# Attention scores as 64-deep products in row halves, and a division moved behind the value product

## The chip, the core and the metric

The kernel runs on one core of one Trainium2 chip. The core has TensorE (PE, with its weight loads as PEld), VectorE (DVE), ScalarE (ACT), GpSimd (POOL) and SyncE (SP), which issues DMA. The metric is the device time of one execution in microseconds, as a median of several. One execution was also recorded by the profiler; the rows below are from that one.

## What is computed

One inference step of a mixer layer: a normalised and modulated input goes through one projection into branches; two of them are a short convolution and a spatial gate, the third is a neighbourhood attention over a 32 x 64 grid of 2048 latent tokens, whose queries also see 128 cached context keys, and 128 prompt tokens that see their own 128 keys. There are 8 heads of 64. The branches are gated, joined and projected back. What matters here is the attention and its gate (without the indexing):

```python
s_loc = einsum(q, k_window) * ATTN_SCALE
s_loc = where(valid, s_loc + bias, NEG_INF)
s_ctx = einsum(q, ctx_k) * ATTN_SCALE
p = softmax(concatenate([s_loc, s_ctx], axis=-1), axis=-1)
out = einsum(p_loc, v_window) + einsum(p_ctx, ctx_v)
yc = out.reshape(bn, n, C_W) * silu(gc)
```

## The kernel before

All matrix products are done in float16 with a high and a low half of each factor, three products for one (high x high, high x low, low x high).

**Stages.** Up to 410 us the kernel normalises the input, computes the spatial gate and the values, and splits the weights. From there to 960 us it works through a list of jobs, one projection of 128 output channels each (`proj`, 24 products per tile of 512 tokens): for each of four head pairs `q`, `k` and the gate `gc`, and between them the convolution branch (`xa`, `ca`, and `ba` with `ga`, the convolution job). From 960 us it does the output projection.

**Attention between the projections.** A head pair's attention has 17 units: 16 blocks of 8 x 16 queries (a window of 352, 480 or 384 keys and the 128 context keys) and the prompt tokens. The steps of a unit don't run in a loop of their own. They are posted with a due time on a modelled clock (`post`), and each projection product advances that clock (`tick`); a step is emitted, in the order of its due time, between two projection products. The table `T` holds the times: `pace` is the distance of two units (6.0, 6.0, 4.9 and 4.7 us for the four head pairs), `a_half` the half pace between the two heads, `a_step` the delays of the steps behind the scores, `a_val` the delay of the value products behind the transposing DMA (5.7, 7.5, 6.2 and 5.6 us). `drain` emits what is still open of a given tag at once. Every engine works through its own instructions in the order in which they were emitted.

**Steps of one head of a unit.** `scores`: the stationary factor `QS` holds the high half of the queries in 64 rows and the low half in the other 64, and `KH` and `KL` hold the keys' halves twice, in both row halves; so a product over 128 rows with `KH` and one with `KL` make all scores (L1028 for the context, L1031 for the window). The second copy of the keys is made by DMA from SBUF to SBUF (L1249, L1250). VectorE adds the bias table `TB` and takes the maximum (L1043). `expo` on ScalarE writes the exponentials in float32 with their sum (L1052), `norm` on VectorE takes the reciprocal (L1055, L1056), `high` on ScalarE writes the normalised probabilities in float16 into one of three buffers `PH` (L1059), `low` on VectorE the rest (L1062), and `turn` issues a transposing DMA from SyncE's queue (L1068). `values` makes the products with `VW` and `v_ctx` in two column halves of the array, one for each head (L1087), and VectorE combines the result with the gate `sgc` (L1095). GpSimd makes the bias tables (`make_tables`, L1002) and the convolution (`conv`, L1182 and L1185).

## Time and profile before

| | |
|---|---|
| median of three runs | 1187.61 us (1185.17 to 1192.42) |
| the profiled execution, its own time | 1188.24 us |
| its span, first to last instruction | 1186.2 us |
| TensorE busy | 1069.7 us, 90% of the span |
| VectorE busy | 843.5 us, 71% |
| ScalarE busy | 447.3 us, 38% |
| GpSimd busy | 346.2 us, 29% |

The shares are means over stages with different limits, so what a change in the attention is worth has to be read from 410 to 926 us, where the attention runs. A busy TensorE counts a product until its results are out; how far apart two products begin tells how much of the queue one takes.

### The profile page before, as it was taken

The page shows a single profiled execution, that of the slowest core. Times are in us where ns is not written, and L with a number is a line of the kernel's source. Part 1 is how long each engine was busy: PE and PEld are TensorE (multiplying, and loading weights), DVE is VectorE, ACT ScalarE, POOL GpSimd, SP SyncE. Part 2 cuts the span into 40 slices and gives each one's busy share as a digit, 9 for nine tenths or more (in the row PEclk, how much of TensorE's full clock was granted, in tenths as well). Part 3 has the DMA queues.
Part 4 walks back from the last instruction along what each step waited for, and adds up shares of the span by engine and source line. Part 5 has one row for each costly group of instructions (what it writes and reads, how often), then busy time and mean ns, then how long its engine had stood idle before and what let it go on. Part 6 is the DMA issues. An engine that isn't in the chain of part 4 may idle for free. (4 is left out here: it accounts for less than half of the span.)

```text
span 1186.2 us, 21036 instructions
## 1 busy us (share of the span) xinstructions
PE 1069.7 (90%) x8044; PEld 681.4 (57%) x8044; DVE 843.5 (71%) x2071; ACT 447.3 (38%) x758; POOL 346.2 (29%) x346
## 2 busy tenths in 40 slices
PE   5588989889968999999999999999988999888885
PEld 1377866477754455554545445545544477776774
DVE  4678866665562389954898549973899658777877
ACT  1432322223332266543655436753666321121111
POOL 0145655200002122102662022300325414334434
PEclk9699999989988999999999999999999999999998
DMA  9713104168957238754666746757476663433341
GB/s 330 260 43 103 59 10 142 54 211 294 308 185 197 77 74 147 130 127 102 113 145 122 152 105 125 150 125 150 97 136 119 198 211 107 144 123 106 120 129 54
DMA packets 254356, 165.50 MB, mean 140 GB/s; under 512 B 163600, under 2 KB 224808, under 8 KB 254256
## 3 DMA queue, kind: packets, MB, share of 16 engines
q1 hardware_dynamic: 254256, 164.16, 53.6%
q8 instruction: 63, 1.03, 0.4%
q14 instruction: 37, 0.30, 0.1%
HBM read 88.06 MB, written 36.21 MB: 105 GB/s over the span
## 5 line engine op out<-in xcount | busy, mean ns | idle before, releaser
L548 PE MATMUL pj<-h_hi,wring 128*128 128x512 f16 (+1 forms) x1280 | 336.2, 349 | 9.2 <-DMA wring<-wj_d 9.2
L548 PEld LDWEIGHTS <-wring 128*128 128x128 f16 x2400 | 211.7, 98 | 224.1 <-DMA wring<-wj_d 9.3
L548 PE MATMUL pj<-h_lo,wring 128*128 128x512 f16 (+1 forms) x640 | 217.9, 349 | 0.0
L1319 PE MATMUL ps<-wo,yh 128*128 128x512 f32 (+1 forms) x840 | 193.5, 390 | 21.0 <-DVE yh L1129 21.0
L1319 PEld LDWEIGHTS ps<-wo,yh 128*128 128x128 f32 x840 | 153.8, 188 | 60.5 <-DVE yh L1129 27.0
L1062 DVE SCALAR_TENSOR_TENSOR PH<-pt,sm,PH 128x608 f16<-128x608 f32 (+3 forms) x136 | 155.3, 1142 | 2.6 <-ACT PH L1059 2.4
L1002 POOL TENSOR_TENSOR TB<-raw,msk 128x480 f32<-128x480 f32 (+2 forms) x96 | 96.2, 1010 | 187.6 <-DVE sm L1043 187.6
L1059 ACT ACTIVATE PH<-pt,sm 128x608 f16<-128x608 f32 (+3 forms) x136 | 99.9, 734 | 95.1 <-ACT pt L1052 62.3
L1052 ACT ACTIVATE pt<-pt,sm,scal 128x608 f32<-128x608 f32 (+2 forms) x128 | 108.3, 846 | 57.6 <-DVE sm L1048 54.0
L1043 DVE CUSTOM_DVE_ANT_0 pt<-s,TB 128x608 f32<-128x608 f32 (+2 forms) x128 | 93.3, 729 | 11.2 <-PE s L1031 10.0
L558 PE MATMUL vvps<-wV,h_hi 128*128 128x256 f16 x544 | 94.0, 277 | 3.6 <-DVE vt L923 3.6
L558 PEld LDWEIGHTS <-h_hi 128*128 128x128 f16 x816 | 82.0, 102 | 23.1 <-issue 11.1
L548 PE MATMUL p<-h_hi,wring 128*128 128x512 f16 (+1 forms) x320 | 85.9, 352 | 1.9 <-DVE th L565 1.9
L1343 ACT ACTIVATE r<-r,omv 128x1024 f32<-128x1024 f32 x16 | 19.9, 1244 | 177.0 <-issue 141.1
L548 PEld LDWEIGHTS <-wB 128*128 128x128 f16 x768 | 63.4, 98 | 24.7 <-issue 1.3
L558 PE MATMUL vvps<-wV,h_lo 128*128 128x256 f16 x272 | 75.3, 277 | 0.0
L1344 POOL TENSOR_TENSOR r<-r,gam 128x1024 f32<-128x1024 f32 x16 | 38.2, 2388 | 126.4 <-ACT r L1343 126.4
L548 PE MATMUL ups<-h_hi,wB 128*128 128x128 f16 (+2 forms) x448 | 70.8, 267 | 0.3 <-DVE wB L238 0.3
L986 POOL TENSOR_SCALAR raw<-raw,scal 128x528 f32<-128x528 f32 x8 | 5.5, 704 | 220.2 <-DVE scal L189 165.8
L1129 DVE TENSOR_TENSOR yh<-yf,yh 128x1024 fp32r<-128x1024 f32 x17 | 41.0, 2410 | 35.2 <-ACT yh L1128 35.2
L1222 DVE SCALAR_TENSOR_TENSOR KL<-pj,scal,KH 64x512 f16<-64x512 f32 (+1 forms) x40 | 26.8, 670 | 54.1 <-ACT KH L1221 53.9
L496 POOL TENSOR_TENSOR h_lo<-hf,h_hi 128x512 f16<-128x512 f32 x34 | 39.9, 1179 | 74.9 <-DMA bsb<-in_b_spatial_dram 42.2
(214 smaller groups left out, 1712.0 us busy)
## 6 DMA issues: line engine op xcount, KB each, us to landing
wa<-in_w_ada_dram SPq DMA_DIRECT2D x24, 512.0 KB, 7.4
wraw<-in_w_in_dram SPq DMA_DIRECT2D x20, 512.0 KB, 5.7
wj_d<-wsp SPq DMA_DIRECT2D x40, 256.0 KB, 6.3
wring<-wj_d SPq DMA_DIRECT2D x20, 512.0 KB, 5.7
yf<-y_d SPq DMA_DIRECT2D x17, 512.0 KB, 5.6
xt<-in_x_sample_dram SPq DMA_DIRECT2D x16, 512.0 KB, 5.0
VW<-v_d SPq DMA_DIRECT2D x64, 128.0 KB, 5.1
xr<-in_x_sample_dram SPq DMA_DIRECT2D x16, 512.0 KB, 4.1
```

The lines of the kernel that those rows point to most:

```text
L496: G.tensor_tensor(out=h_lo[:, k0:k0 + g, t0:t0 + n], in0=hv, in1=hi, op=ALU.subtract)
L548: PE.matmul(out=ps, lhsT=w(a, k) if callable(w) else w[:, a, k, :], rhs=mov(b, k), start=(k == 0 and i == 0), stop=(k == KB - 1 and i == 2))
L558: PE.matmul(out=ps, lhsT=a[:, k, i * P:(i + 1) * P], rhs=w[:, b, k, :], start=(k == 0 and q == 0), stop=(k == KB - 1 and q == 2))
L1002: G.tensor_tensor(out=TB[:, tslot(u) + h, P:P + n], in0=raws[h][:, off:off + n], in1=msk[:, mo:mo + n], op=ALU.add)
L1043: V.tensor_tensor_reduce(out=pt[:, :w], in0=src, in1=TB[:, tslot(u) + h, 0:w], op0=ALU.add, op1=ALU.max, scale=1.0, scalar=-3e38, accum_ou ...
L1052: S.activation(out=pt[:, :w], in_=src, func=AF.Exp, bias=sm[:, 1:2], scale=st_["isig"], accum_out=sm[:, 2:3])
L1059: S.activation(out=pb[:, 0:w], in_=pt[:, :w], func=AF.Copy, scale=sm[:, 3:4])
L1062: V.scalar_tensor_tensor(out=pb[:, wp:wp + w], in0=pt[:, :w], scalar=sm[:, 3:4], in1=pb[:, 0:w], op0=ALU.mult, op1=ALU.subtract)
L1129: V.tensor_tensor(out=yh[:, 1], in0=yf, in1=yh[:, 0].bitcast(F32), op=ALU.subtract)
L1222: V.scalar_tensor_tensor(out=KL[a, h, t0:t0 + n], in0=ps[a], scalar=ckk[a], in1=KH[a, h, t0:t0 + n], op0=ALU.mult, op1=ALU.subtract)
L1319: PE.matmul(out=ps, lhsT=yh[:, a, k, :], rhs=wo[:, b, k, f0:f1], start=(k == 0 and q == 0), stop=(k == KB - 1 and q == 2))
L1344: G.tensor_tensor(out=r, in0=r, in1=gam, op=ALU.mult)
```

## The change

Queries and keys are kept once each, both heads of a pair one above the other in the 128 rows, as `QH`, `QL`, `KH`, `KL`. The scores of a unit are made for both heads together, each in three products over the 64 rows of its half of the array; the two heads' products alternate. The second copy of the keys and its DMAs go, and the copies out of the projections for Q and K cover 128 partitions in one operation in place of two of 64.

The probabilities aren't normalised any more before the value product. The exponent gets ln(2 to the power of 14) added; `high` is an exponential that writes float16, `expo` makes the same in float32 with the sum, and `low` is their difference, on GpSimd for the first head of a pair and on VectorE for the second. Per unit there is one reciprocal of both sums; GpSimd spreads it over a 128x128 tile `rq`, TensorE transposes that behind the value products, VectorE multiplies it with the gate (`gq`) and that with the value products. The modelled clock counts three passes for the scores of a unit, and `a_step` has four delays in place of five.

```diff
-    a_step=(700.0, 700.0, 2100.0, 2750.0, 3700.0),
+    a_step=(700.0, 750.0, 2700.0, 3300.0),
...
+LN14 = 14.0 * float(np.log(2.0))
...
-    QS = ap.tile([P, 2, TOK], F16, name="QS")
-    KH = ap.tile([P, 2, TOK + CTX], F16, name="KH")
-    KL = ap.tile([P, 2, TOK + CTX], F16, name="KL")
+    QH = ap.tile([P, TOK], F16, name="QH")
+    QL = ap.tile([P, TOK], F16, name="QL")
+    KH = ap.tile([P, TOK + CTX], F16, name="KH")
+    KL = ap.tile([P, TOK + CTX], F16, name="KL")
...
+                post(T['a_start'][hp] + u * pace, lambda u=u: self.scores(u), ("as", hp, u))
                 for h in range(2):
-                    post(T['a_start'][hp] + (u + T['a_half'] * h) * pace, lambda u=u, h=h: self.scores(u, h), ("as", hp, u))
-
-        def scores(self, u, h):
-            i = 2 * u + h
-            drain(("a", self.hp, i - T['a_guard']), ("at", self.hp, u))
-            tg = ("a", self.hp, i)
-            sm = ap.tile([P, 4], F32, name="sm", bufs=8)
-            s = aps.tile([P, 2, 512], F32, name="s", tag="s", bufs=2)
+                    post(T['a_start'][hp] + (u + T['a_half'] * h) * pace, lambda u=u, h=h: self.soft(u, h), ("as", hp, u))
+
+        def scores(self, u):
+            drain(("a", self.hp, 2 * u - T['a_guard']), ("at", self.hp, u))
+            n = 0
             if u < 16:
                 rb, j = UNITS[u]
                 nr = RB_NROW[rb]
                 n = 32 * nr
-                q = QS[:, h, u * P:(u + 1) * P]
-                for e, kk in enumerate((KH, KL)):
-                    PE.matmul(out=s[:, 0, 384:512], lhsT=q, rhs=kk[:, h, TOK:TOK + CTX], start=(e == 0), stop=(e == 1))
-                for e, kk in enumerate((KH, KL)):
-                    win = kk[:, h, RB_ROW0[rb] * 64:(RB_ROW0[rb] + nr) * 64].rearrange("p (r c) -> p r c", c=64)
-                    PE.matmul(out=s[:, 1, 0:n], lhsT=q, rhs=win[:, :, COL0[j]:COL0[j] + 32], start=(e == 0), stop=(e == 1))
-            else:
-                n = 0
-                q = QS[:, h, LAT:TOK]
-                for e, kk in enumerate((KH, KL)):
-                    PE.matmul(out=s[:, 0, 384:512], lhsT=q, rhs=kk[:, h, LAT:TOK], start=(e == 0), stop=(e == 1))
-            now[0] += 2 * (P + n) / 2.4
+            t0 = u * P
+            s = [aps.tile([P, 2, 512], F32, name="s", tag="s", bufs=2) for h in range(2)]
+            pairs = ((QH, KH), (QL, KH), (QH, KL))
+            for e, (q, kk) in enumerate(pairs):
+                for h in range(2):
+                    a = slice(64 * h, 64 * h + 64)
+                    k0 = TOK if u < 16 else LAT
+                    PE.matmul(out=s[h][:, 0, 384:512], lhsT=q[a, t0:t0 + P], rhs=kk[a, k0:k0 + CTX], start=(e == 0), stop=(e == 2))
+            if u < 16:
+                for e, (q, kk) in enumerate(pairs):
+                    for h in range(2):
+                        a = slice(64 * h, 64 * h + 64)
+                        win = kk[a, RB_ROW0[rb] * 64:(RB_ROW0[rb] + nr) * 64].rearrange("p (r c) -> p r c", c=64)
+                        PE.matmul(out=s[h][:, 1, 0:n], lhsT=q[a, t0:t0 + P], rhs=win[:, :, COL0[j]:COL0[j] + 32],
+                                  start=(e == 0), stop=(e == 2))
+            now[0] += 3 * (P + n) / 2.4
+            self.ss[u] = s
...
+            if h == 0:
+                self.sums[u] = ap.tile([P, 4], F32, name="sums", bufs=5)
+            total = self.sums[u]
+            s = self.ss[u][h]
...
-            V.tensor_scalar(out=sm[:, 1:2], in0=sm[:, 0:1], scalar1=st_["isig"], scalar2=-1.0, op0=ALU.mult, op1=ALU.mult)
+            V.tensor_scalar(out=sm[:, 1:2], in0=sm[:, 0:1], scalar1=st_["nisig"], scalar2=LN14, op0=ALU.mult, op1=ALU.add)
             pb = PH[:, i % 3]
 
+            def high():
+                S.activation(out=pb[:, 0:w], in_=src, func=AF.Exp, bias=sm[:, 1:2], scale=st_["isig"])
+
             def expo():
-                S.activation(out=pt[:, :w], in_=src, func=AF.Exp, bias=sm[:, 1:2], scale=st_["isig"], accum_out=sm[:, 2:3])
-
-            def norm():
-                V.tensor_scalar(out=sm[:, 2:3], in0=sm[:, 2:3], scalar1=2.0 ** -14, scalar2=None, op0=ALU.mult)
-                V.reciprocal(out=sm[:, 3:4], in_=sm[:, 2:3])
-
-            def high():
-                S.activation(out=pb[:, 0:w], in_=pt[:, :w], func=AF.Copy, scale=sm[:, 3:4])
+                S.activation(out=pt[:, :w], in_=src, func=AF.Exp, bias=sm[:, 1:2], scale=st_["isig"], accum_out=total[:, h:h + 1])
 
             def low():
-                V.scalar_tensor_tensor(out=pb[:, wp:wp + w], in0=pt[:, :w], scalar=sm[:, 3:4],
-                                       in1=pb[:, 0:w], op0=ALU.mult, op1=ALU.subtract)
+                (G if h == 0 else V).tensor_tensor(out=pb[:, wp:wp + w], in0=pt[:, :w], in1=pb[:, 0:w], op=ALU.subtract)
+                if h == 1:
+                    V.reciprocal(out=total[:, 2:4], in_=total[:, 0:2])
+                    r = ap.tile([P, P], F32, name="rq", bufs=4)
+                    for e in range(2):
+                        G.tensor_scalar(out=r[:, 64 * e:64 * e + 64], in0=ones[:, 0:64], scalar1=total[:, 2 + e:3 + e], scalar2=1.0,
+                                        op0=ALU.mult, op1=ALU.mult)
+                    self.rs[u] = r
 
             def turn():
                 drain(("av", self.hp, u - T['av_guard']))
@@ -1070,12 +1090,13 @@
                 if h == 1:
                     post(T['a_val'][self.hp], lambda: self.values(u, [self.ts.pop((u, e)) for e in range(2)], wp // P, n), ("av", self.hp, u))
 
-            for f, at in zip((expo, norm, high, low, turn), T['a_step']):
+            for f, at in zip((high, expo, low, turn), T['a_step']):
...
-            o = aps.tile([P, P], F32, name="o", tag="o")
+            o = aps.tile([P, 2, P], F32, name="o", tag="o")
+            rt, o = o[:, 1], o[:, 0]
...
+            PE.transpose(rt, self.rs.pop(u), ident)
             now[0] += nch * 3 * 80.0
+            t0 = u * P
+            gq = ap.tile([P, P], F32, name="gq", bufs=2)
+            V.scalar_tensor_tensor(out=gq, in0=rt, scalar=st_["cpv"], in1=sgc[:, t0:t0 + P], op0=ALU.mult, op1=ALU.mult)
             if u < 16:
                 rb, j = UNITS[u]
                 if j == 0:
                     self.ys = yst.tile([P, 8, 64], F32, name="yc", tag="yst")
-                V.scalar_tensor_tensor(out=self.ys[:, :, j * 16:j * 16 + 16], in0=o.rearrange("p (r c) -> p r c", c=16),
-                                       scalar=st_["cpv"], in1=sgc[:, u * P:(u + 1) * P].rearrange("p (r c) -> p r c", c=16),
-                                       op0=ALU.mult, op1=ALU.mult)
+                V.tensor_tensor(out=self.ys[:, :, j * 16:j * 16 + 16], in0=o.rearrange("p (r c) -> p r c", c=16),
+                                in1=gq.rearrange("p (r c) -> p r c", c=16), op=ALU.mult)
...
-                S.activation(out=QS[0:64, 0, t0:t0 + n], in_=ps[0:64], func=AF.Copy, scale=cq[0:64])
-                S.activation(out=QS[64:128, 1, t0:t0 + n], in_=ps[64:128], func=AF.Copy, scale=cq[64:128])
-                V.scalar_tensor_tensor(out=QS[64:128, 0, t0:t0 + n], in0=ps[0:64], scalar=cq[0:64],
-                                       in1=QS[0:64, 0, t0:t0 + n], op0=ALU.mult, op1=ALU.subtract)
-                V.scalar_tensor_tensor(out=QS[0:64, 1, t0:t0 + n], in0=ps[64:128], scalar=cq[64:128],
-                                       in1=QS[64:128, 1, t0:t0 + n], op0=ALU.mult, op1=ALU.subtract)
+                S.activation(out=QH[:, t0:t0 + n], in_=ps, func=AF.Copy, scale=cq)
+                V.scalar_tensor_tensor(out=QL[:, t0:t0 + n], in0=ps, scalar=cq, in1=QH[:, t0:t0 + n],
+                                       op0=ALU.mult, op1=ALU.subtract)
             elif kind == "k":
-                for h in range(2):
-                    a = slice(64 * h, 64 * h + 64)
-                    S.activation(out=KH[a, h, t0:t0 + n], in_=ps[a], func=AF.Copy, scale=ckk[a])
-                    V.scalar_tensor_tensor(out=KL[a, h, t0:t0 + n], in0=ps[a], scalar=ckk[a], in1=KH[a, h, t0:t0 + n],
-                                           op0=ALU.mult, op1=ALU.subtract)
-                rng = {1: (0, 1024), 3: (1024, 2048)}.get(ti)
...
-                if rng:
-                    r = slice(*rng)
-                    for kk in (KH, KL):
-                        SP.dma_start(out=kk[64:128, 0, r], in_=kk[0:64, 0, r])
-                        SP.dma_start(out=kk[0:64, 1, r], in_=kk[64:128, 1, r])
...
-            st_["cpv"] = mul(mul(inv_v[idx // 2], wgc["c"]), const=2.0 ** -15)
+            st_["cpv"] = mul(mul(inv_v[idx // 2], wgc["c"]), const=0.5)
+            st_["nisig"] = mul(st_["isig"], const=-1.0)
```

TensorE, a unit of the first head pair with 480 window columns, before: the products of one head between two projection products.

```order
L548 MATMUL pj<-h_hi,wring 128x512
L1028 LDWEIGHTS QS
L1028 MATMUL s<-KH,QS 128x128
L1028 LDWEIGHTS QS
L1028 MATMUL s<-KL,QS 128x128
L1031 LDWEIGHTS QS
L1031 MATMUL s<-KH,QS 128x480
L1031 LDWEIGHTS QS
L1031 MATMUL s<-KL,QS 128x480
L548 LDWEIGHTS wring
```

The other head's four stand half a pace later, again between two projection products.

TensorE, such a unit of the first head pair, after: the end of the twelve score products of both heads, and what follows them.

```order
L1042 LDWEIGHTS QL
L1042 MATMUL s<-KH,QL 128x480
L1042 LDWEIGHTS QH
L1042 MATMUL s<-KL,QH 128x480
L1042 LDWEIGHTS QH
L1042 MATMUL s<-KL,QH 128x480
L1108 LDWEIGHTS v_ctx
L1108 MATMUL o<-ptr,v_ctx 64x128
L1108 LDWEIGHTS v_ctx
L1108 MATMUL o<-ptr,v_ctx 64x128
```

Two groups of four full-size products are now one group of twelve half-height ones, in which the heads alternate, and in this head pair the value products of an earlier unit follow at once, with no projection product between.

TensorE, the end of a unit's value products, after (`rq` holds the reciprocals, `o` the value products).

```order
L1108 LDWEIGHTS VW
L1108 MATMUL o<-ptr,VW 64x128
L1111 MATMUL o<-ident,rq 128x128
L549 LDWEIGHTS wring
L549 MATMUL pj<-h_hi,wring 128x512
```

The transposition stands between the value products and the next projection product; before, that product followed directly.

GpSimd, second head pair, around one block of the convolution (`cvt` and `c` are its tiles, `raw` holds the bias), before:

```order
L1002 TENSOR_TENSOR TB<-raw_5978,msk 128x480
L1002 TENSOR_TENSOR TB<-raw_5980,msk 128x480
L1182 TENSOR_SCALAR cvt<-z,conv_sb 128x512
L1182 TENSOR_SCALAR c_6588<-z,conv_sb 128x512
L1185 TENSOR_TENSOR cvt<-cvt,c_6588 128x512
L1182 TENSOR_SCALAR c_6591<-z,conv_sb 128x512
L1185 TENSOR_TENSOR cvt<-cvt,c_6591 128x512
L1002 TENSOR_TENSOR TB<-raw_5978,msk 128x480
L1002 TENSOR_TENSOR TB<-raw_5980,msk 128x480
L1002 TENSOR_TENSOR TB<-raw_5978,msk 128x480
```

The block had only the bias tables as neighbours.

GpSimd, second head pair, around one block of the convolution, after:

```order
L1076 TENSOR_TENSOR PH<-pt,PH 128x480
L1004 TENSOR_TENSOR TB<-raw_6072,msk 128x480
L1004 TENSOR_TENSOR TB<-raw_6074,msk 128x480
L1081 TENSOR_SCALAR rq<-ones,sums 128x64 x2
L1206 TENSOR_SCALAR cvt<-z,conv_sb 128x512
L1206 TENSOR_SCALAR c_6692<-z,conv_sb 128x512
L1209 TENSOR_TENSOR cvt<-cvt,c_6692 128x512
L1206 TENSOR_SCALAR c_6695<-z,conv_sb 128x512
L1209 TENSOR_TENSOR cvt<-cvt,c_6695 128x512
L1076 TENSOR_TENSOR PH<-pt,PH 128x608
L1081 TENSOR_SCALAR rq<-ones,sums 128x64 x2
L1076 TENSOR_TENSOR PH<-pt,PH 128x608
```

The low halves (`PH`) and the spread reciprocals (`rq`) have joined the tables and the convolution in this queue.

## Rows read from the trace of the kernel before

**Rows 1.** Stretches: length, busy us (instructions) of PE, PEld, DVE, ACT, POOL; granted clock, DMA, GB/s.

```profile
410.00:515.00 105.00, 104.13 (x937) 56.58 (x935) 87.59 (x229) 61.76 (x113) 23.84 (x25) 1.00 0.62 113
...
555.00:661.00 106.00, 103.50 (x927) 56.25 (x926) 90.58 (x239) 60.60 (x111) 47.73 (x48) 0.98 0.62 117
...
703.00:794.00 91.00, 86.84 (x830) 47.66 (x828) 82.97 (x226) 61.82 (x113) 21.81 (x22) 1.00 0.67 129
...
831.00:926.00 95.00, 86.33 (x824) 47.39 (x824) 87.68 (x231) 58.37 (x107) 35.55 (x36) 0.98 0.62 118
```

**Rows 2.** Waits of TensorE from 410 to 927 us: total, times, longest.

```profile
PE o L1087 <- DMA ptr<-PH: 17.7, 17, 2.5
```

**Rows 3.** Timeline of TensorE, first head pair: start us, us, line, operation, form, count.

```profile
443.58 0.22 PE L1028 MATMUL s<-KH,QS 128*128 128x128 f16 x1
443.64 0.22 PE L1028 MATMUL s<-KL,QS 128*128 128x128 f16 x1
443.70 0.37 PE L1031 MATMUL s<-KH,QS 128*128 128x480 f16 x1
...
444.10 0.59 PE L548 MATMUL pj<-h_hi,wring 128*128 128x512 f16 x2
...
444.75 0.59 PE L548 MATMUL pj<-h_hi,wring 128*128 128x512 f16 x2
445.27 0.36 PE L1087 MATMUL o<-ptr,v_ctx 128*64 128x128 f16 x6
...
446.07 0.39 PE L548 MATMUL pj<-h_lo,wring 128*128 128x512 f16 x1
```

**Rows 4.** Timeline of TensorE at a row-split pair, during the spatial-gate stage.

```profile
102.87 0.27 PE L548 MATMUL ups<-h_hi,wB 128*128 128x256 f16 x1
103.07 0.38 PE L208 MATMUL ax<-scal,ones 2*128 2x2 f32 x2
103.38 0.28 PE L548 MATMUL ups<-h_hi,wB 128*128 128x256 f16 x1
```

**Rows 5.** Timeline of TensorE at a transposition inside the projections.

```profile
410.74 0.27 PE L1240 MATMUL kps<-ident,kp 128*128 128x128 f32 x1
410.85 0.38 PE L548 MATMUL pj<-h_hi,wring 128*128 128x512 f16 x1
```

**Rows 6.** Groups of VectorE: busy us, mean ns of one, idle before and its releaser.

```profile
L1062 DVE SCALAR_TENSOR_TENSOR PH<-pt,sm,PH 128x608 f16<-128x608 f32 (+3 forms) x136 | 155.3, 1142 | 2.6 <-ACT PH L1059 2.4
...
L1095 DVE SCALAR_TENSOR_TENSOR yc<-o,scal,sgc 128x128 f32<-128x128 f32 x64 | 21.9, 342 | 3.5 <-PE o L1087 3.4
...
L1055 DVE TENSOR_SCALAR sm<-sm 128x1 f32<-128x1 f32 x136 | 19.9, 146 | 16.1 <-ACT pt L1052 15.1
```

**Rows 7.** Timeline of VectorE's low halves and GpSimd, 442 to 446 us.

```profile
442.22 1.10 POOL L1002 TENSOR_TENSOR TB<-raw,msk 128x480 f32<-128x480 f32 x1 [1.87 <-DVE sm L1043]
...
442.31 1.66 DVE L1062 SCALAR_TENSOR_TENSOR PH<-pt,sm,PH 128x608 f16<-128x608 f32 x1
...
445.73 0.84 DVE L1062 SCALAR_TENSOR_TENSOR PH<-pt,sm,PH 128x608 f16<-128x608 f32 x1
```

**Rows 8.** Groups of GpSimd, shapes apart.

```profile
L496 POOL TENSOR_TENSOR h_lo<-hf,h_hi 128x512 f16<-128x512 f32 x34 | 39.9, 1179 | 74.9 <-DMA bsb<-in_b_spatial_dram 42.2 <-DVE h_hi L493 9.0 <-DVE mv L270 8.1
...
L1182 POOL TENSOR_SCALAR c<-z,conv_sb 128x128 f32<-128x128 f32 x4 | 1.5, 370 | 0.2
```

**Rows 9.** A stretch under the convolution job of the second head pair, columns as in rows 1.

```profile
573.00:620.00 47.00, 44.50 (x402) 23.95 (x401) 42.13 (x104) 27.60 (x49) 34.69 (x31) 0.96 0.63 124
```

**Rows 10.** Timeline of GpSimd: first and last of the five operations of one tile's convolution.

```profile
598.34 1.24 POOL L1182 TENSOR_SCALAR cvt<-z,conv_sb 128x512 f32<-128x512 f32 x1
...
603.09 1.27 POOL L1185 TENSOR_TENSOR cvt<-cvt,c 128x512 f32<-128x512 f32 x1
```

**Rows 11.** Exponential at full width (groups of ScalarE), and landing of the transposing DMAs.

```profile
L1052 ACT ACTIVATE pt<-pt,sm,scal 128x608 f32<-128x608 f32 x64 | 57.1, 892 | 24.0 <-DVE sm L1048 23.3
...
DMA to landing us min/median/max: 2.3/3.4/4.9
```

More of the change, by code (lines that the diff above doesn't have):

```diff
@@ L1227, in hybrid_step @@
                     PE.transpose(cps, ckt, ident)
-                    for h in range(2):
-                        a = slice(64 * h, 64 * h + 64)
-                        S.activation(out=KH[a, h, TOK:], in_=cps[a], func=AF.Copy, scale=s_k[a])
-                        V.scalar_tensor_tensor(out=KL[a, h, TOK:], in0=cps[a], scalar=s_k[a], in1=KH[a, h, TOK:],
-                                               op0=ALU.mult, op1=ALU.subtract)
+                    S.activation(out=KH[:, TOK:], in_=cps, func=AF.Copy, scale=s_k)
+                    V.scalar_tensor_tensor(out=KL[:, TOK:], in0=cps, scalar=s_k, in1=KH[:, TOK:],
+                                           op0=ALU.mult, op1=ALU.subtract)
                 if ti == 4:
-                    rng = (2048, TOK + CTX)
                     kp = tmpA.tile([P, P], F32, name="kp", tag="th")
```

13 lines of the change are left out of this document (12 added, 1 removed).

## The prediction

> **What bounds the kernel now.** I read the table of stretches first, then the waits of TensorE, then the timeline of one unit of attention, and last the groups of VectorE and GpSimd. The change touches only the four head pairs of attention, which run between 410 and 926 us. In the table of stretches [rows 1] the reader is to see that TensorE is busy for nearly all of each stretch: 104.13 of 105 us in the first, 103.50 of 106 in the second, 86.84 of 91 in the third and 86.33 of 95 in the fourth. So the bound is TensorE's queue, in which projections, scores and value products stand one behind the other; a microsecond added to that queue is a microsecond of time. What TensorE idles in them comes to 0.9 + 2.5 + 4.2 + 8.7 = 16.3 us. Over 410 to 927 us 17 waits, 17.7 us in all, stand before the first value product of a unit, which waits for the transposing DMA of the probabilities [rows 2]. That DMA is late because VectorE is: busy for 82.97 of 91 us in the third stretch and 87.68 of 95 in the fourth [rows 1]. So the change can gain in two places, the length of the queue and these waits.
>
> **Scores.** One head of a unit with 480 window columns has two products of 128 columns and two of 480; they begin at 443.58 and the next projection at 444.10, so they take 0.52 us, of which the 480-column ones take 0.20 each (443.70 to 444.10) [rows 3]. That is 0.417 ns a column. Per head pair the sixteen units have 6784 window columns and 2048 of cached context and the prompt unit has 128: 8960 columns, times four head pairs 35840. Before, four such passes (two per head): 143360 columns, 59.8 us. After, three passes for each of two heads. If the two heads' products in the two row halves run side by side, it is 107520 columns, 44.8 us: **-15.0 us**. If they run one behind the other it is 89.6 us: +29.8 us. No row shows half-height products side by side. The nearest one shows half-width ones: a unit of 352 window columns has four chunks of six value products of 128 columns, 24 in all, and they take 0.80 us from 445.27 to 446.07 [rows 3]. In single file they would take 24 times 0.053 to 0.06 (443.58 to 443.64), at least 1.28 us; in pairs half of that, 0.64 to 0.72 us. So half-width pairs run side by side, and I take it that half-height ones do.
>
> **The change of shape.** The value products also show what it costs to leave the full-size array and come back. Projections are 0.21 apart, but after the second of the two that begin at 444.75 (so at 444.96) the first value product begins only at 445.27, 0.10 later than its turn; and the 0.80 us are 0.08 to 0.16 more than 12 pairs need [rows 3]. That is 0.18 to 0.26 us a visit; I take 0.22. Before, scores are full-size and pay nothing of this. After, each of the 68 units makes one more visit: 68 x 0.22 = 15.0 us. In the first head pair the order puts the values of a unit directly behind the scores of a later one, with no full-size product between, which saves one of the two changes, 0.11 us, about 14 times: 1.5 us. Sum **+13.5 us**. Lower end: the one visit to a row-split array, two small products with one or two rows of contraction, comes in with 0.20 us from the start of a 256-column product, which itself needs 256 x 0.417, 0.11, so 0.09 is lost; then 0.31 go by with both products and the way out [rows 4]. If nothing of that is lost, a visit costs 0.09, in all 6 us. Upper end: before each pair two sets of weights must be loaded; if those are not hidden under the 128-column pairs, such a pair lasts as long as two products, 3 x 0.053 x 68 = 10.8 us more.
> The Trainium skill bears on this: "TensorEngine Tiling (Array Packing)", section Theoretical Speedup, gives up to 2x for a contraction of 64, and its section Key Properties says that a change of the tiling mode drains the engine. The first alone would make this edit -15 us, the second takes nearly all of it back; the 0.22 us of the value visits agree with the second.
>
> **The transposition of the reciprocals.** Each unit gets one more float32 128x128 transposition on TensorE. The one of the new keys takes 0.11 us from its start to that of the next projection (410.74 to 410.85) [rows 5]: 68 x 0.11 = **+7.5 us**. It stands between the value products and the projection, so it shares their way back.
> TensorE's queue therefore becomes -15.0 + 13.5 + 7.5 = **+6.0 us** longer, between about -1 (cheap changes of shape) and +17 (uncovered loads).
>
> **VectorE.** Per unit go one low half of 1.142 us (the other head's is moved), two scalings of 0.146, one of two reciprocals of about the same length [rows 6], and the old combination with the gate, 0.342, becomes two such operations [rows 6]. The low half that stays takes 0.84 us alone and 1.66 where a table operation runs on GpSimd beside it (442.22 to 443.32) [rows 7]; I take 1.4 in place of 1.142, because GpSimd will be busier. Sum per unit -1.14 - 0.29 - 0.15 + 0.34 + 0.26 = -1.0 us, ends -1.5 and -0.7. In the fourth stretch VectorE has 87.68 / 17 = 5.2 us a unit in 5.6 us; after that 4.2. So the waits that come of VectorE's backlog go: all of the third stretch's 4.2 us, and some 3 of the fourth's 8.7. The halved number of copies for Q and K frees VectorE and ScalarE only between the stretches, where TensorE waits for neither; I cost it, and the removed key copies by DMA (SyncE queues them there too), at nothing, since no TensorE wait names them [rows 2].
>
> **GpSimd.** It gets the low half of the first head and two 128x64 operations a unit. The same kind of subtraction takes 1.179 us for 512 columns [rows 8]; with the mean width of 8960 / 17 = 527 that is 1.21 us. The 128x64 operations lie below the 0.37 us of a 128x128 one [rows 8]; I take 0.28 each. Together 1.8 us a unit. Where no convolution runs it has room: in the third stretch 21.81 of 91 us are busy [rows 1] and 17 x 1.8 = 31 come in. But between 573 and 620 us, under the convolution job, it is busy for 34.69 of 47 us [rows 9] with some seven units (106 / 17 = 6.2 us each in this stretch), and 7 x 1.8 = 12.6 makes 47.3: full. A tile's convolution is a block of five operations from 598.34 to 604.36, 6.0 us [rows 10], and the low half of a first head that is queued behind it is late by up to that. Behind the low half wait, in SyncE's queue, this head's transposing DMA and all after it, then the value products. The same follows from the order in the fourth head pair.
> A second thing tightens. PH has three buffers; before, one is held from the high half on ScalarE to the landing of the DMA. The change fills it before the full exponential, so it is held longer by that operation, 0.89 us at the widest [rows 11]. The hold was the high half (no longer than the exponential), the low half and the landing, 0.89 + 1.14 + 3.4 = 5.4 us [rows 6, 11]; it becomes some 6.3 to 7. Three heads are 1.5 units, 8.4 us in the fourth stretch, so it fits until GpSimd is late by more than about 1.5 us. And scores of a unit now need both score buffers, the second freed half a pace before; VectorE, at 4.2 of 5.6 us, can do that.
> So of 16.3 us of idle, some 7 go and, as I estimate, about as much comes back: four or five convolution blocks in the second stretch and three in the fourth, about 1 us each beyond the slack that the values' delay leaves. Net **0**, ends -15 and +20.
>
> **Sum.** The profiled execution took 1188.24 us (span 1186.2), 0.6 above the median of 1187.61. 1188.2 + 6.0 + 0 = **1194 us**, half a per cent slower, which lies within the 1% that a measurement of this kernel can hardly tell from no change.
>
> **Rivals.** (a) *The waits simply vanish*: VectorE was their only cause and GpSimd's blocks are covered by the 5.6 to 7.5 us that the schedule leaves between a transposing DMA and its values. Then 13 to 15 us of idle go, and the granted clock, 0.98 in two stretches [rows 1], becomes full, worth up to 2 us in each (2% of 106 and of 95), of which I count half: 1188 + 6 - 15 - 2 = 1177, with the cheap changes of shape 1170. For it speaks that all 17 waits name the same DMA, against it the full GpSimd. It alone ends on the faster side.
> (b) *GpSimd becomes the bound of the convolution job*: the 47.3 us of work in 47 leave out that it waits, in order, for each unit's exponential on ScalarE and reciprocal on VectorE; at 1 us for each of the seven units it needs 54 us, 115%. Then PH's three buffers pass the delay on to ScalarE, and idle grows by 15 to 20 us: 1188 + 6 + 18 = 1212. It decides from the point at which a tile's block and its units' work on GpSimd, with these waits, last longer than the tile's projections and products on TensorE.
> (c) *The halves don't run side by side*: scores +29.8 instead of -15.0, so 1194 + 45, less some 10 of waits covered by the longer queue: 1229.
> (d) *Loads uncovered under the short pairs*: 1194 + 11 = 1205.
>
> **How the numbers follow.** Forecast 0.48, with about 8 us to both sides, 1186 to 1202, of which a fifth lies above 1199.5; (a) 0.22, half of it under 1175.7; (b) 0.17; (c) 0.07; (d) 0.06. Faster by over 1%: 0.11. Slower by over 1%: 0.10 + 0.17 + 0.07 + 0.06 = 0.40. Within 1%: 0.49. The range leaves out the better half of (a) and (c): 1176 to 1220.
>
> **What would show it.** Right: score pairs of 480 columns 0.20 us apart with the two heads' starts together, some 0.1 us lost on both sides of a visit, one transposition of 0.11 us a unit, VectorE about 4.2 us a unit, GpSimd's busy time near 465 us, few waits of TensorE in the third stretch and those that remain beside the convolution blocks. Wrong: score products 0.20 us apart in single file (c), waits of ScalarE for PH's DMA or of TensorE in every convolution tile (b), or under 5 us of TensorE idle in all between 410 and 926 us (a).

## The result, and the profile after

The changed kernel takes **1197.53 us** (median of 8 runs, 1196.58 to 1201.91), the kernel before on the same chip 1188.43 us: 1.0085 times as long, 95% interval 1.0066 to 1.0105. The forecast was 1194, "half a per cent slower, which lies within the 1%", with a range from 1176 to 1220. The profiled execution took 1196.58 us (span 1194.8). Medians and ratios, here and below, leave out the executions in a slow state, such as one of 1812.88 us.

The engines of the whole kernel after, from the page (busy us, share of the span, instructions):

```profile
PE 1076.8 (90%) x8376; PEld 672.5 (56%) x8376; DVE 710.7 (59%) x1827; ACT 430.6 (36%) x714; POOL 462.6 (39%) x550
```

TensorE's busy time rose by 7.1 us (it was 1069.7), VectorE's fell by 133 us (843.5), GpSimd's rose by 116 us (346.2). So VectorE lost about a sixth of its work, and the kernel didn't get faster. The same four stretches as in [rows 1], a little later in the program, with the same columns:

```profile
410.00:516.00 106.00, 105.92 (x1023) 54.89 (x1022) 61.05 (x177) 63.84 (x112) 53.43 (x70) 1.00 0.63 115
555.00:667.00 112.00, 106.54 (x1012) 53.71 (x1007) 65.08 (x189) 63.64 (x110) 72.31 (x94) 1.00 0.59 115
706.00:799.00 93.00, 89.87 (x909) 45.66 (x908) 56.35 (x175) 63.34 (x111) 49.18 (x69) 1.00 0.72 127
835.00:930.00 95.00, 87.58 (x887) 44.36 (x886) 60.81 (x175) 59.42 (x104) 59.18 (x79) 0.98 0.61 115
```

TensorE is still what is busy nearly all the time. In the second, third and fourth stretch it idles 5.5, 3.1 and 7.4 us, in the first next to nothing. Its waits from 400 to 975 us (total, times, longest) answer to [rows 2]:

```profile
PE s L1036 <- DVE sm L1061: 8.8, 10, 3.3
PE o L1108 <- DMA ptr<-PH: 7.0, 7, 2.9
PE p L549 <- DVE cvt L1219: 3.7, 1, 3.7
PE o L1108 <- DVE yc L1120: 1.2, 2, 0.8
PE p L549 <- DVE th L566: 0.8, 1, 0.8
```

The waits for the transposing DMA fell from 17.7 to 7.0 us. In their place the scores (L1036) wait 8.8 us for VectorE's maximum (L1061), which frees a score buffer. All waits together are 21.5 us; in the same stretch of before they were 17.7 for the DMA and 2.8 for others, 20.5. So idle time is +1.0, busy time +7.1, and that is the 8 to 9 us of the result.

The timeline of TensorE at one unit of the first head pair, as [rows 3], and the end of the scores of another unit, which a projection follows:

```profile
443.67 0.59 PE L549 MATMUL pj<-h_hi,wring 128*128 128x512 f16 x2
444.19 0.23 PE L1036 MATMUL s<-KH,QH 64*128 64x128 f16 x2
...
444.37 0.37 PE L1042 MATMUL s<-KH,QH 64*128 64x480 f16 x2
444.57 0.37 PE L1042 MATMUL s<-KH,QL 64*128 64x480 f16 x2
444.78 0.37 PE L1042 MATMUL s<-KL,QH 64*128 64x480 f16 x2
445.07 0.36 PE L1108 MATMUL o<-ptr,v_ctx 128*64 128x128 f16 x6
445.26 0.67 PE L1108 MATMUL o<-ptr,VW 128*64 128x128 f16 x18
445.87 0.33 PE L1111 MATMUL o<-ident,rq 128*128 128x128 f32 x1
446.03 0.38 PE L549 MATMUL pj<-h_lo,wring 128*128 128x512 f16 x1
...
855.48 0.37 PE L1042 MATMUL s<-KL,QH 64*128 64x480 f16 x2
855.78 0.23 PE L549 MATMUL pj<-h_lo,wring 128*128 128x128 f16 x1
```

Three things stand here. A row of two (x2) is one product of each head; such pairs follow at 0.06 us (128 columns) and 0.20 us (480), as single products did before, so the heads do run side by side and their weight loads are hidden. The way in costs 0.09 us (the second projection of 443.67 began at 443.885; the scores come 0.31 after it in place of 0.216), the way out 0.09 (445.07 is 0.29 after the last pair, which needs 0.20), or 0.10 where a projection follows (855.78 is 0.30 after the last pair). And the transposition takes 0.16 us from its start to the next projection, not 0.11 as in [rows 5].

The groups of the low halves and of the spread reciprocals (busy us, mean ns of one, idle before and its releasers), 400 to 975 us, answer to [rows 6, 8]:

```profile
L1076 POOL TENSOR_TENSOR PH<-pt,PH 128x608 f16<-128x608 f32 (+3 forms) x68 | 81.1, 1193 | 58.0 <-ACT pt L1073 56.1 <-DVE sm L1066 1.6
L1076 DVE TENSOR_TENSOR PH<-pt,PH 128x608 f16<-128x608 f32 (+3 forms) x68 | 55.3, 814 | 49.3 <-ACT pt L1073 48.9
L1081 POOL TENSOR_SCALAR rq<-ones,sums 128x64 f32<-128x64 f32 x136 | 41.1, 317 | 121.8 <-DVE sums L1078 109.7 <-PE o L1111 5.8 <-PE s L1042 2.6
```

GpSimd takes 1.19 us for a low half for which VectorE now takes 0.81, and it stands 121.8 us at the reciprocals, mostly for VectorE, with the next operations queued behind. The longest score wait (3.26 us at 864.05) can be followed back in the timelines of GpSimd, ScalarE and VectorE at the start of the fourth head pair:

```profile
846.60 0.79 ACT L1073 ACTIVATE pt<-pt,sm,scal 128x480 f32<-128x480 f32 x1
...
850.01 1.10 POOL L1004 TENSOR_TENSOR TB<-raw,msk 128x480 f32<-128x480 f32 x1 [1.80 <-DVE sm L1061]
851.07 1.10 POOL L1076 TENSOR_TENSOR PH<-pt,PH 128x480 f16<-128x480 f32 x1
...
856.82 0.79 ACT L1070 ACTIVATE PH<-pt,sm,scal 128x480 f16<-128x480 f32 x1 [3.26 <-POOL PH L1076]
...
859.13 0.69 DVE L1265 SCALAR_TENSOR_TENSOR sgc<-sgc,pj 128x512 f32<-128x512 f32 x1 [4.36 <-ACT sgc L1264]
...
863.00 0.29 DVE L1265 SCALAR_TENSOR_TENSOR sgc<-sgc,pj 128x128 f32<-128x128 f32 x1 [1.59 <-ACT sgc L1264]
863.21 0.78 DVE L1061 CUSTOM_DVE_ANT_0 pt<-s,TB 128x608 f32<-128x608 f32 x1
...
864.05 0.21 PE L1036 MATMUL s<-KH,QH 64*128 64x128 f16 x1 [3.26 <-DVE sm L1061]
```

GpSimd reaches the low half of one head only at 851.07, 3.7 us after the exponential of that head (847.39): ahead of it in the queue stands a bias table, which itself waits 1.80 us for VectorE. The transposing DMA of this head is issued at 852.20 and lands at 856.72, 4.5 us later, where the median is 3.5. ScalarE's high half three heads on needs the same PH buffer and stands 3.26 us for it, until 856.82. (The bracket names a low half on GpSimd that ended at 856.75; that one belongs to another buffer.) ScalarE works in order, so the gate's tanh behind it is late; VectorE stands 4.36 us for that and 1.59 us for the next tanh, and behind these stands the maximum that TensorE waits for. In all ScalarE stands 40.8 us for PH behind the DMA after the change, before it 0.4. Over all units but those of the prompt a PH buffer is held for 7.6 us on average, from the start of the high half to the landing of the DMA; before, it was 6.1. The exponential that now lies in between makes 1.0 us of the difference.

### The profile page after: what moved, and what is told of

The parts are those of the page before. It is cut to its first block, busy times and chain, and to the rows that moved or that the text cites. A ratio compares the mean times of both kernels' runs of the same rounds, so it can differ in the third digit from the quotient of the medians.

```text
span 1194.8 us, 21531 instructions
## 1 busy us (share of the span) xinstructions
PE 1076.8 (90%) x8376; PEld 672.5 (56%) x8376; DVE 710.7 (59%) x1827; ACT 430.6 (36%) x714; POOL 462.6 (39%) x550
## 5 line engine op out<-in xcount | busy, mean ns | idle before, releaser
L549 PEld LDWEIGHTS <-wring 128*128 128x128 f16 x2400 | 216.4, 100 | 234.3 <-issue 28.2
L1070 ACT ACTIVATE PH<-pt,sm,scal 128x608 f16<-128x608 f32 (+2 forms) x128 | 107.9, 843 | 141.3 <-DVE sm L1066 69.1
L1061 DVE CUSTOM_DVE_ANT_0 pt<-s,TB 128x608 f32<-128x608 f32 (+2 forms) x128 | 92.7, 724 | 32.6 <-PE s L1042 29.5
L1076 POOL TENSOR_TENSOR PH<-pt,PH 128x608 f16<-128x608 f32 (+3 forms) x68 | 81.1, 1193 | 58.0 <-ACT pt L1073 56.1
L1081 POOL TENSOR_SCALAR rq<-ones,sums 128x64 f32<-128x64 f32 x136 | 41.1, 317 | 121.8 <-DVE sums L1078 109.7
L1076 DVE TENSOR_TENSOR PH<-pt,PH 128x608 f16<-128x608 f32 (+3 forms) x68 | 55.3, 814 | 49.3 <-ACT pt L1073 48.9
```

What stands on the lines that cost most here:

```text
L549: PE.matmul(out=ps, lhsT=w(a, k) if callable(w) else w[:, a, k, :], rhs=mov(b, k), start=(k == 0 and i == 0), stop=(k == KB - 1 and i == 2))
L1061: V.tensor_tensor_reduce(out=pt[:, :w], in0=src, in1=TB[:, tslot(u) + h, 0:w], op0=ALU.add, op1=ALU.max, scale=1.0, scalar=-3e38, accum_ou ...
L1070: S.activation(out=pb[:, 0:w], in_=src, func=AF.Exp, bias=sm[:, 1:2], scale=st_["isig"])
L1076: (G if h == 0 else V).tensor_tensor(out=pb[:, wp:wp + w], in0=pt[:, :w], in1=pb[:, 0:w], op=ALU.subtract)
L1081: G.tensor_scalar(out=r[:, 64 * e:64 * e + 64], in0=ones[:, 0:64], scalar1=total[:, 2 + e:3 + e], scalar2=1.0, op0=ALU.mult, op1=ALU.mult)
```

## The experiments

The theories. **A**: the waits that came start at the ring of three PH buffers. **B**: they start at GpSimd, which reaches its part late. **C**: the longer queue of TensorE is all that counts. **D**: the second score buffer comes free too late. **E** to **K** stand with their runs. All ratios are against the kernel before on the same chip; each kernel was also profiled.

### Four PH buffers (A against B)

```diff
-    PH = ap.tile([P, 3, 2 * 640], F16, name="PH")
+    PH = ap.tile([P, 4, 2 * 640], F16, name="PH")
-            pb = PH[:, i % 3]
+            pb = PH[:, i % 4]
```

> The changed kernel with four probability buffers PH in place of three. Theory A (ring): of the 16 us that TensorE waits for VectorE and the transposing DMA in attention after the change, the waits of the scores for VectorE's maximum (8.8 us) start with ScalarE's high half, which stands 3 us and more for its PH buffer (40.8 us in all). A fourth buffer takes most of that: ScalarE's waits for PH fall below 10 us, TensorE's score waits below 3 us, 1197 becomes 1189 to 1192. Rival B (GpSimd's own work is the cause, the low half is late in any buffer): the value products wait instead, the time stays at 1195 to 1199. Rival C (the length of TensorE's queue is all there is): idle shrinks but the time stays, 1195 to 1198.

Measured: 1194.43 us, ratio 1.0049 (1.0031 to 1.0067), between the numbers of A and those of B and C. ScalarE's waits for the DMA behind PH fell from 40.8 to 1.0 us, as A said, but TensorE's waits for the scores did not fall below 3 us:

```profile
PE s L1036 <- DVE sm L1061: 6.8, 7, 1.9
PE o L1108 <- DMA ptr<-PH: 5.1, 5, 1.3
```

The 3.26 us at 864 became 1.89 at 859.87. With the waits at the ring gone, most of TensorE's waits stay. So the ring is a part, worth about 3 us (the two intervals just touch), not the root.

### Both low halves on VectorE (B)

```diff
-                (G if h == 0 else V).tensor_tensor(out=pb[:, wp:wp + w], in0=pt[:, :w], in1=pb[:, 0:w], op=ALU.subtract)
+                V.tensor_tensor(out=pb[:, wp:wp + w], in0=pt[:, :w], in1=pb[:, 0:w], op=ALU.subtract)
```

> The changed kernel with the low halves of both heads on VectorE. Rival B (GpSimd's blocks are the cause of the waits that came): GpSimd's busy time falls by about 81 us to 380, the waits beside the convolution blocks go and 1197 becomes 1188 to 1192. Theory A (ring): VectorE takes some 0.9 us more a unit (3.6 becomes 4.5 in the last head pair, of 5.6), the hold of a PH buffer gets no longer than before, ScalarE's waits for PH fall from 40.8 to 10 to 25 us and the time comes to 1192 to 1197. If VectorE becomes late again, as it was before the change, the waits for the DMA grow from 7 back to 12 or more and the time is 1197 to 1203.

Measured: **1187.18 us**, ratio 0.9986 (0.9970 to 1.0003), some 10 us less than the change. VectorE is busy for 759.2 us in place of 710.7, GpSimd for 390.5 in place of 462.6. TensorE's waits:

```profile
PE s L1036 <- DVE sm L1061: 6.1, 6, 1.9
PE p L549 <- DVE cvt L1219: 2.2, 1, 2.2
PE p L549 <- DVE th L566: 2.2, 1, 2.2
PE o L1108 <- DMA ptr<-PH: 1.7, 2, 1.5
```

The DMA waits fell from 7.0 to 1.7 us although VectorE has more to do; all waits are 13.0 us against 21.5. B is borne out: the low half on GpSimd cost more than it relieved. The time lies 0.8 us under B's range. A's number, 1192 to 1197, failed, though ScalarE's waits for PH behind the DMA fell to 23.2 us, within the 10 to 25 that A gave.

### GpSimd's low half only where no convolution runs

```diff
-                (G if h == 0 else V).tensor_tensor(...)
+                (G if h == 0 and self.hp in (0, 2) else V).tensor_tensor(...)
```

> The changed kernel with GpSimd's low half only in the first and third head pair, where no convolution runs on GpSimd; in the second and fourth both low halves are VectorE's. Theory B (the low half is late because it stands behind the convolution's blocks on GpSimd): the same gain as with both low halves on VectorE everywhere, 1186 to 1190, the waits in the second and fourth stretch go. Rival H (the low half costs in every pair, because GpSimd takes 1.19 us for what VectorE does in 0.81): about half the gain, 1191 to 1194.

Measured: 1192.67 us, ratio 1.0049 (1.0026 to 1.0071): somewhere between a third of the gain (by the ratios) and a half (by the medians), and within the numbers of H. So the convolution's blocks alone, which the forecast blamed, don't explain the loss; behind tables that themselves wait, as at 850.01 above, the low half is late too. The trace doesn't settle the share of each: against the run before this one its waits are 0.8 us shorter in the second head pair, 0.6 longer in the third and 3.5 longer in the fourth, where the two kernels do the same.

### The spread reciprocals on VectorE

```diff
-                        G.tensor_scalar(out=r[:, 64 * e:64 * e + 64], in0=ones[:, 0:64], ...
+                        V.tensor_scalar(out=r[:, 64 * e:64 * e + 64], in0=ones[:, 0:64], ...
```

> The changed kernel with the 128x64 operations that spread the reciprocals on VectorE; the low half of the first head stays on GpSimd. Rival I (GpSimd is late because it stands in order for VectorE's reciprocals, 109.7 us in 45 waits, with the convolution and the next low half queued behind): the waits for the DMA and the scores fall from 16 to below 8 us, 1197 becomes 1188 to 1191. Theory B (the low half behind the convolution's blocks is enough): GpSimd's busy time falls by 41 us, the waits stay at 11 us and more, 1194 to 1198.

Measured: 1204.06 us, ratio 1.0134 (1.0116 to 1.0151). Both numbers missed; it got worse:

```profile
PE s L1036 <- DVE sm L1061: 15.1, 19, 3.0
PE o L1108 <- DMA ptr<-PH: 3.4, 3, 2.3
```

The DMA waits did fall, to 3.4 us, but the score waits rose from 8.8 to 15.1, now in the first stretch too. The two operations (0.36 us each) stand in VectorE's queue ahead of the maximum that frees a score buffer. Whether it costs anything that GpSimd stands for the reciprocals isn't shown by this, since the edit also lengthens VectorE's queue; what VectorE does ahead of a maximum does cost. Why 0.72 us a unit weigh more here than the 0.8 of a low half did two runs above stays open.

### The second head's maximum earlier (D)

```diff
-    a_half=0.5,
+    a_half=0.3,
```

> The second head's maximum follows the first one's after 0.3 of a pace in place of 0.5, in the changed kernel. Rival D (the score buffer of the second head comes free too late because its reading is put half a pace later, and now both are needed at once): the 8.8 us of score waits go, 1197 becomes 1188 to 1191. Theory A (the ring of PH is the root): the PH buffers are asked for earlier, so ScalarE's waits for PH grow from 40.8 us and the time stays at 1196 to 1201.

Measured: 1210.79 us, ratio 1.0176 (1.0153 to 1.0198). Score waits 6.1 us, little less than 8.8, but the waits for the DMA rose from 7.0 to 16.0 (18 times). D's number fell, and so did A's: the time lies beyond 1201, and ScalarE's waits for PH behind the DMA shrank from 40.8 to 17.2 us. The edit has a second effect: the values are posted from the second head's DMA, so they came 0.2 of a pace (about 1 us) earlier too, and that can account for the DMA waits; it isn't shown. A form without this effect is tried below.

### The scores alone (E, F, G)

The products, buffers and copies of Q and K of the change, with the normalisation, the value products and the five steps of the kernel before:

```diff
-    a_step=(700.0, 750.0, 2700.0, 3300.0),
+    a_step=(700.0, 700.0, 2100.0, 2750.0, 3700.0),
...
-            for f, at in zip((high, expo, low, turn), T['a_step']):
+            for f, at in zip((expo, norm, high, low, turn), T['a_step']):
...
-            PE.transpose(rt, self.rs.pop(u), ident)
```

> Only the scores of the change: two heads in row halves, three 64-deep products each; the normalisation stays before the value products as in the kernel before, without the transposition and without GpSimd's part. Theory E (sum of the terms): TensorE's queue is 15 us shorter by columns and about 12.5 us longer by changes of shape, so 2.5 us shorter than before, VectorE is as busy as before and the DMA waits of some 17 us return: 1184 to 1192, no difference from before that counts. Rival F (the row halves are what cost, the rest is free): about 1197. Rival G (the row halves gain all of their 15 us): about 1173.

Measured: 1202.12 us, ratio 1.0109 (1.0085 to 1.0133): no faster than the whole change (the intervals overlap), 10 us above E's range and nearest to F's 1197. The same kernel once more:

> The kernel with the scores of the change alone, once more, for one look: 24 us of score waits and about 1202 again.

Measured: 1204.01 us, with 23.8 us of score waits. The largest of TensorE's waits in the first of the two:

```profile
PE s L1036 <- DVE sm L1058: 24.3, 32, 1.8
```

TensorE is busy for 1073.9 us, less than in the change (1076.8), which has the transposition as well, but more than in the kernel before (1069.7): the queue 2.5 us shorter that E expected doesn't show. Part of that is the count, since a product ahead of a wait is busy until its results are out (0.22 us for one of 128 columns, where the next can follow after 0.06), and there are 37 waits here in place of 20. The DMA waits of the kernel before did not return; 24 us of score waits came. A unit now asks for both score buffers at once, and the second is freed by the maximum of the second head. With the old normalisation VectorE stands 78 times, 53.9 us in all, for ScalarE's exponential before it can scale the sum (33 times and 15.1 us in the kernel before), with that maximum behind it in order. J or K?

```diff
-    a_half=0.5,
+    a_half=0.3,
-    a_val=(5700.0, 7500.0, 6200.0, 5600.0),
+    a_val=(6900.0, 8700.0, 7180.0, 6540.0),
```

> The kernel with the scores of the change alone, with the second head's maximum 0.3 of a pace behind the first one's in place of 0.5, and the values posted later by as much, so that they keep their distance to the scores. Theory J (the next unit's scores need both score buffers, and the second comes free only half a pace before): the 24 us of score waits fall below 10, 1202 becomes 1188 to 1194. Rival K (VectorE and ScalarE wait for one another in order, twice a head in the old normalisation, and that sets when the second buffer comes free): the waits stay near 20 us and the time at 1199 to 1205.

Measured: 1218.73 us, ratio 1.0259 (1.0245 to 1.0274). The score waits are 25.9 us, and VectorE's waits for the exponential rose to 92.2 us (113 times). J fell; K has the waits right, but the time lies beyond it, with 7.4 us of DMA waits as well. So a shorter distance in the schedule alone doesn't free the second buffer earlier; that VectorE's waits ahead of the maximum do it fits the numbers, but is argued. What the other normalisation is worth beside paired scores can be read from two runs that both have all low halves on VectorE: this kernel with the old one takes 1202.12 us, the run above with the new one 1187.18, and the score waits are 24.3 against 6.1 us. So the normalisation behind the value product pays for the coupling that the paired scores bring. Normalisation alone, beside full-height scores, was not tried.

### The scores head by head

```diff
-            for e, (q, kk) in enumerate(pairs):
-                for h in range(2):
+            for h in range(2):
+                for e, (q, kk) in enumerate(pairs):
```

(and the window products of a head behind its context products, then the other head)

> The changed kernel with the same score products in another order: all of one head's, then all of the other's, so that no product of the other row half stands directly behind one of the first. If the 15 us of the scores come of two halves that run side by side (the forecast's term), the 480-column products stand 0.20 us apart one by one, a unit of 480 columns takes some 0.75 us more and the 68 units 35 to 45 us more in the queue, less some 8 us of waits that it covers: 1197 becomes 1222 to 1240. If the order of issue doesn't matter to the halves (the array takes the other half's product forward, or the gain was not from there), 1195 to 1200.

Measured: 1204.8 us, ratio 1.0140 (1.0096 to 1.0185), 7 us above the change: between the two numbers, much nearer to the second. The timeline of such a unit:

```profile
446.59 0.23 PE L1036 MATMUL s<-KH,QH 64*128 64x128 f16 x1
446.66 0.22 PE L1036 MATMUL s<-KH,QL 64*128 64x128 f16 x1
446.72 0.22 PE L1036 MATMUL s<-KL,QH 64*128 64x128 f16 x1
446.72 0.23 PE L1036 MATMUL s<-KH,QH 64*128 64x128 f16 x1
446.77 0.36 PE L1040 MATMUL s<-KH,QH 64*128 64x480 f16 x1
...
446.97 0.49 PE L1040 MATMUL s<-KH,QL 64*128 64x480 f16 x2
...
447.60 0.36 PE L1106 MATMUL o<-ptr,v_ctx 128*64 128x128 f16 x6
```

In the program the first head's three window products (L1040) stand ahead of the second head's first context product (L1036). Here that one starts at 446.72, ahead of the first window product at 446.77: the halves run as two streams, and the second starts two products after the first. Products and way out take 1.01 us (446.59 to 447.60) against 0.88 (444.19 to 445.07) in pairs; 0.13 x 68 = 8.8 us of queue is what alternating them is worth. TensorE's busy time rose by 11.6 us (to 1088.4), and its waits of 21.5 us fell to 16.1.

### Without the transposition, and with it in another place

```diff
-            PE.transpose(rt, self.rs.pop(u), ident)
+            rt = self.rs.pop(u)
```

This kernel leaves the transposition out; the gate is multiplied by the reciprocals as they stand.

> The changed kernel without the transposition of the reciprocals on TensorE; VectorE combines the gate with the untransposed reciprocals, so the normalisation of the output is left out in its right form and all else is done. The forecast put the transposition at 0.11 us, 7.5 in all; the trace after shows 0.165 between its start and the next product. If 0.165 is what it costs: 68 x 0.165 = 11 us less queue, 1186 if the waits stay as they are, 1190 if a third of it turns into waits. If it costs 0.11: 1190 to 1194. If it was hidden (weights loaded ahead, under the value products): 1196 to 1198.

Measured: 1191.79 us, ratio 1.0045 (1.0021 to 1.0070). TensorE's busy time fell by 11.6 us (1076.8 to 1065.2). By the rows it should be 68 x 0.165 = 11.2; the agreement is better than the count, since 2.6 us of the fall lie before 400 us, where the two kernels do the same. 6 us reach the end; 4.5 became waits, mostly of the scores (13.4 us in place of 8.8). The time alone lies among the numbers given for 0.11 us; what speaks for 0.165 is the rows. Then the transposition stays and is put, with VectorE's use of it, 100 ns of schedule later, which is behind the next projection product:

```diff
-            PE.transpose(rt, self.rs.pop(u), ident)
+            def gated():
+                PE.transpose(rt, self.rs.pop(u), ident)
+                ...
+            post(100, gated, ("ar", hp, u))
```

> The changed kernel with the transposition of the reciprocals, and what VectorE does with it, put behind the next projection product in place of directly behind the value products. If the 0.165 us come of its place right behind the column-split value products, it falls to 0.11 between two full-size products and 68 x 0.055 = 3.7 us go: 1193 to 1195. If a float32 transposition of reciprocals costs 0.165 in any place: 1196 to 1199.

Measured: 1192.94 us, ratio 1.0022 (0.9999 to 1.0045). In the timeline:

```profile
446.84 0.39 PE L549 MATMUL pj<-h_lo,wring 128*128 128x512 f16 x1
447.06 0.27 PE L1115 MATMUL o<-ident,rq 128*128 128x128 f32 x1
447.17 0.59 PE L549 MATMUL pj<-h_hi,wring 128*128 128x512 f16 x2
```

Between two projections it takes 0.11 us, as in [rows 5]; directly behind the value products it took 0.16. So its place costs 0.05 us a unit, 3.4 us in all, of the 4.6 that this run gained. TensorE's waits fell too, from 21.5 to 19.2 us.

### What the runs point to, together

Both low halves on VectorE, four PH buffers, the later transposition, and VectorE's part of the gate's evacuation 3 us later, out of the way of the maximum:

```diff
+    gate=3000.0,
...
-                V.scalar_tensor_tensor(out=sgc[:, t0:t0 + n], ...)
+                post(T['gate'], lambda t0=t0, n=n, ps=ps: V.scalar_tensor_tensor(
+                    out=sgc[:, t0:t0 + n], ...), ("ag",))
```

> The changed kernel with four edits that the runs point to: both low halves on VectorE (1187.2 by itself), four PH buffers, the transposition behind the next projection product (about 3 us of queue), and VectorE's part of the gate's evacuation posted 3 us later, so that the maximum of the second head doesn't stand behind ScalarE's queue at the start of the third and fourth head pair (two waits of 1.9 us and some of 0.5). If the gains add up: 1187 - 3 - 4 = 1180, between 1177 and 1184. If the waits only move: 1184 to 1188.

Measured: **1175.31 us**, ratio 0.9900 (0.9883 to 0.9917), under the range that it was given. TensorE's waits from 400 to 975 us are 6.6 us in all, and the scores wait no more:

```profile
PE p L550 <- DVE cvt L1225: 2.2, 1, 2.2
PE p L550 <- DVE th L567: 1.7, 1, 1.7
PE o L1110 <- DVE yc L1124: 1.7, 2, 1.1
PE o L1110 <- DMA ptr<-PH: 1.0, 2, 0.8
```

With these four edits the changed form is 1% faster than the kernel before. Four PH buffers and the later evacuation of the gate are no part of the change and were not tried in the kernel before, so how much of the 1% is the change's own stays open; with both low halves on VectorE as the only edit it is level with the kernel before (0.9986). Which of the four edits is worth what beyond the runs above was not separated. TensorE's busy time, too, is 10.8 us below that of the change (1066.0), of which the place of the transposition explains some 3.

## Why the prediction was right, step by step

- **Scores, -15.0 us: right.** Pairs of 480 columns stand 0.20 us apart with the loads hidden; rivals (c) and (d) are out. What the term leaned on, half-width pairs of [rows 3], carried over.
- **Change of shape, 0.22 us a visit: nearly.** 0.09 in and 0.09 to 0.10 out in the timeline above; I count 0.19: 68 x 0.19 = 12.9 less 1.2 for the dozen units whose values follow directly, 11.7 in place of 13.5. That the array is left and entered at a price agrees with the drain at a change of tiling mode in the Trainium skill ("TensorEngine Tiling (Array Packing)", Key Properties).
- **Transposition, 0.11 us, "+7.5": mis-sized.** 0.165 us (median over the units) and 11.2 in all. [Rows 5] show it between full-size projections, and here it stands behind column-split products; the run with its place changed gives 0.11 again. The two errors cancel in part: -15.0 + 11.7 + 11.2 = +7.9 against the forecast +6.0; the page's busy time says +7.1.
- **VectorE, -1.0 us a unit: too small.** 60.81 us for 17 units are 3.6 us a unit in the fourth stretch, not 4.2, so 1.6 less than the 5.2 before. I took 1.4 us for the low half that stays, because of GpSimd; it takes 0.81. This term set no part of the sum.
- **GpSimd, "near 465 us": right** (462.6). "Full" under the convolution job was too much: from 573 to 620 us it is busy for 38.83 of 47 us, not 47.3. That a low half is late there came true: in the second head pair the longest delay of a first head's low half behind its exponential is 8.0 us, where it was 2.1. Rival (b) came by its sign, not by its size: the three PH buffers do pass the delay on to ScalarE (40.8 us for PH's DMA), but TensorE's idle time grew by 1.0 us, not by 15 to 20.
- **Idle, "net 0, ends -15 and +20": +1.0, right as a sum, in its parts by luck.** The DMA waits that went are 10.7 us, not 7; 8.5 came for the scores, 2.6 at the end of the convolution and some small ones. The third stretch, whose 4.2 us were all to go, still idles 3.1. The forecast placed the new waits beside the convolution's blocks; that is only half of it. What came is mostly a wait that the forecast had named and costed at nothing: "scores of a unit now need both score buffers, the second freed half a pace before; VectorE, at 4.2 of 5.6 us, can do that". VectorE had the time, but it works in order, and in the longest wait, followed back above, the maximum stood behind operations that waited for ScalarE, which waited for PH, whose DMA had waited for GpSimd. The part of the PH ring was seen rightly, and is worth some 3 us; its hold was put too low, before (5.4 us for 6.1) as after (6.3 to 7 for 7.6), because the sum left out the time between the steps.
- **Rival (a)**, that the waits simply vanish, came about with other edits only: with both low halves on VectorE and no other change 8.5 of 21.5 us go, with four edits 15.

## What to carry to other kernels

Half-height products of two heads run side by side and save columns, but count each visit of TensorE to another shape (here 0.19 us) and each small instruction on the way back; keep a transposition away from such a visit by one full-size product. When two results are produced at once that were produced in turn, ask what frees the second buffer, and what stands ahead of that in its engine's queue: the share of busy time won't tell. Moving work to an idle engine helps only if what waits for it can wait for that engine's whole queue.

## What the runs showed of the hardware

Products in the two row halves need not alternate in the program to run side by side: issued head by head, a product of the other half started at 446.72, ahead of three that stand before it in the program and start at 446.77 and later, and the whole cost 7 us in place of the 25 to 43 expected. That different tiles work in parallel stands in the Trainium skill ("TensorEngine Tiling (Array Packing)", Key Properties); the runs add that the program need not alternate them. That every engine works through its instructions in the order in which they were emitted thus holds for these products only within one half. A float32 transposition of 128x128 directly behind column-split products takes 0.165 us, one full-size product later 0.11.
